# Attention visits of two query blocks in a hybrid convolution and attention step

## Chip, cores and metric

The kernel runs on one core of one Trainium2 chip. The metric is the device time of one execution in microseconds; three executions before gave 949.36, 948.08 and 947.59 (median 948.08). TensorE (PE) does matrix products and transposes, VectorE (DVE), ScalarE (ACT) and GpSimd (POOL) the elementwise work, SyncE (SP) issues most loads. Products land in PSUM, of which a tile of 128 partitions x 512 float32 columns is one bank.

## The reference

One layer for two groups of tokens that share all weights: 128 context tokens ("prompt") and 512 latent tokens on a grid of 8 x 64. Each layer projects its modulated input, runs a gated long convolution (branch A) and attention of 16 heads of 64 channels (branch B), gates, merges and normalises. The change touches branch B alone:

```python
def context_attention(q, k, v):
    s = jnp.einsum("bqhd,bkhd->bhqk", q, k).astype(jnp.float32) * (HEAD_DIM ** -0.5)
    p = jax.nn.softmax(s, axis=-1).astype(v.dtype)
    return jnp.einsum("bhqk,bkhd->bqhd", p, v).reshape(B, L, H * Dh)

def neighbourhood_attention(q, k, v, ctx_k, ctx_v, rpb):
    ...
    s_win = jnp.where(in_win[None, None, None], s_win + bias[None].astype(jnp.float32), NEG_INF)
    s_ctx = jnp.einsum("brqhd,bkhd->bhrqk", qg, ctx_k).astype(jnp.float32) * scale
    p = jax.nn.softmax(jnp.concatenate([s_win, s_ctx], axis=-1), axis=-1).astype(v.dtype)
    o = (jnp.einsum("bhrqk,brkhd->brqhd", p[..., :n_slab], vg)
         + jnp.einsum("bhrqk,bkhd->brqhd", p[..., n_slab:], ctx_v))
    return o.reshape(B, L, H * Dh)
...
p_a = (y_a * jax.nn.silu(g_a)) @ w_ba
```

A latent query sees a window of 16 columns in all 8 grid rows, with a learned bias, and all 128 cached context keys in the same softmax. A context query sees the 128 context keys.

## The kernel before

All work is float32. A weight tile is loaded (`raw`), split by ACT and VectorE into a high and a low part (`wh`, `wl`, L92 and L93), and a projection (`proj`, L154) accumulates three products of 128 x 320 for each of 8 input slices into two PSUM banks (`ps_mm`, two such pairs). One of its steps is 6 matmuls; a projection is 8 steps. The values projection is longer (L680, L689).

Attention goes by pairs of heads, called heads here: `j` = 0 to 7, each of 128 channels, two heads `h` on partitions 0 to 63 and 64 to 127. The latent grid is reordered into 8 blocks of 64 tokens; 128 queries at a time are a query block, `b` = 0 to 3, and `n = 4 j + b` counts query blocks from 0 to 31. The window of a block with its context keys has 320 (b = 0, 3) or 384 columns (b = 1, 2).

- `tiled(n)` (L789) first takes two PSUM tiles `s` and records the scores (L741): for b = 0 also the prompt's, into columns 384 to 511 of the same tiles. Then `probs` (L750): VectorE adds bias and mask and takes the minimum in one custom instruction (L757; the scores are negated, so the minimum is the softmax's maximum), ACT takes the exponential with its sum (L760), VectorE the reciprocal (L761), POOL normalises (L762). The result lies in tiles `p` (5 buffers) or `edge` (b = 0 and 3).
- The same visit then records the values (L785) of block `n - 2`, 6 products for two heads over three chunks of 128 keys, into columns of a PSUM tile `o` that lives for a whole head; with block 0 also the prompt's values into `op`. When block 3 is in, VectorE multiplies `o` with the gate `sg` into `ya` (L839, L840).
- `turned(n)` (L843) transposes the probabilities of block `n - 1` (L778; with block 0 the prompt's, L849) into a PSUM tile `pt` for each head, and ACT copies them to `pts` (L780, L851; 4 buffers).

`s`, `o`, `op`, `pt` and `ptp` all come from `ps_ax`, four banks with one tag `aux`. TensorE's order is that of recording (`manual_schedule`); the other engines' orders and the buffer of each tile are chosen by a scheduler from simulated times. Instructions of different engines on one bank of a tile are kept in recording order.

`weave` (L62) mixes the visits into projections: `attend(j)` yields one visit or transposition, `mains(j)` one projection step, and after each step as many visits follow as the ratio `N_ATT` : `n_main` allows. With 24 steps and `N_ATT` = 8 there is a visit or a transposition after every third step. The projections woven in (`mains`, L889) are those needed two heads later: gate `sg` (two buffers, `gate_a`, L864), queries, keys and values, whose tiles (`slot`) are shared by heads two apart. Head 7 is woven with `mix_h` (L869). After the last gating, ACT and VectorE split all 8 tiles of `yh` and `ya` (L934 and below) for the branch projections.

Of the kernel before, what the change touches and what calls it, by code (L numbers as in the profile page):

```python
# [9 lines left out]
F32 = mybir.dt.float32  # L10
F32R = mybir.dt.float32r
AF = mybir.ActivationFunctionType
ALU = mybir.AluOpType
# [3 lines left out]
LP = 128  # L17
LS = 512
NK = 8
NT = 640  # L20
HALF = 320
PC = 0
SC = 128
B7, B01 = slice(128, 192), slice(192, 320)
# [9 lines left out]
KP = slice(768, 896)  # L34
# [5 lines left out]
def tile_hyena_natten_step(ctx: ExitStack, tc: tile.TileContext, a, o):  # L40
    nc = tc.nc
    P = 128
# [7 lines left out]
    def two(t):  # L50
        return t.rearrange("p (a b) -> p a b", a=2)
# [36 lines left out]
    def aux(name):  # L88
        return ps_ax.tile([P, 512], F32, tag="aux", name=name)
# [81 lines left out]
    out = {"yh": {}}  # L171
# [290 lines left out]
    def quarter_head(q):  # L462
        us = []
        out[f"u{q}"] = us
        for i in range(2):
            n = 2 * q + i
            u = hw.tile([P, NG + 1], F32, tag="u", bufs=4, name=f"u{n}")
            x1 = hwa.tile([P, NG + 1], F32, tag="cv", bufs=2, name=f"x1_{n}")
            yield from conv_tile(n, u)
            yield  # L470
            yield from conv_tile(8 + n, x1)
            nc.vector.tensor_tensor(u[:, :NG], u[:, :NG], x1[:, :NG], op=ALU.mult)
            us.append(u)
            yield
# [142 lines left out]
    def chain(*gens):  # L617
        for g in gens:
            yield from g
# [4 lines left out]
    head = quarter_head(0)  # L624
# [82 lines left out]
    ya, tms, edges, biases = [], [], {}, {}  # L707
# [21 lines left out]
    at = mask = None  # L729

    def bias_tile(hd):
        tb = at.tile([P, 256], F32, tag="tb", bufs=2, name=f"tb{hd}")
        load_to(tb[:], a["rpbT"][hd])
        tm = tms[hd % 4]
        nc.gpsimd.tensor_tensor(tm[:, :192], mask[:, :192], tb[:, 64:], op=ALU.subtract)
        nc.gpsimd.tensor_tensor(two(tm[:, 320:832])[:, :, :P], two(mask[:, 192:448]), two(tb[:]), op=ALU.subtract)
        nc.gpsimd.tensor_tensor(tm[:, 832:], mask[:, 448:], tb[:, :192], op=ALU.subtract)
        return tm

    def score(dst, q, k, h):  # L740
        nc.tensor.matmul(dst, q[rows(h)], k[rows(h)], start=True, stop=True, skip_group_check=True)  # L741
# [8 lines left out]
    def probs(j, b, s, tm):  # L750
        lo, hi = TWIN[b]
        res = []
        for h in range(2):
            p = edges[b, h] if b in (0, 3) else at.tile([P, 384], F32, tag="p", bufs=5, name=f"p{j}_{h}_{b}")
            pv = p[:, LIVE[b]]
            sm = at.tile([P, 3], F32, tag="sm", bufs=8, name=f"sm{j}_{h}_{b}")
            nc.vector.tensor_tensor_reduce(  # L757
                pv, s[h][:, : hi - lo], tm[h][:, lo:hi], 1.0, 3.0e38, ALU.add, ALU.min, accum_out=sm[:, 0:1]
            )
            nc.scalar.activation(pv, pv, AF.Exp, scale=-1.0, bias=sm[:, 0:1], accum_out=sm[:, 1:2])  # L760
            nc.vector.reciprocal(sm[:, 2:3], sm[:, 1:2])  # L761
            nc.gpsimd.tensor_scalar_mul(pv, pv, sm[:, 2:3])  # L762
            res.append(p)
        return res
# [8 lines left out]
    def transposed(j, b, ps):  # L773
        res = []
        for h in range(2):
            pt = aux(f"pt{j}_{h}_{b}")
            for i, (_, c) in enumerate(CHUNKS[b]):
                nc.tensor.transpose(pt[:, i * P : i * P + P], ps[h][:, c : c + P], ident[:])  # L778
            ptS = at.tile([P, 384], F32, tag="pts", bufs=4, name=f"pts{j}_{h}_{b}")
            nc.scalar.activation(ptS[:], pt[:, :384], AF.Copy)  # L780
            res.append(ptS)
        return res

    def pvm(dst, lhs, rhs, start, stop):
        nc.tensor.matmul(dst, lhs, rhs, start=start, stop=stop, skip_group_check=True)  # L785

    head = {}

    def tiled(n):  # L789
        j, b = divmod(n, 4)  # L790
        if n < 4 * NK:
            if b == 0:
                cv = at.tile([P, P], F32, tag="cacheV", bufs=2, name=f"cv{j}")
                load_to(cv[:], a["cv"][:, j * P : j * P + P])
                head[j] = dict(cv=cv, tm=biases.pop(j))
            st_ = head[j]
            s = [aux(f"s{b}_{j}_{h}") for h in range(2)]
            if b == 0:
                for h in range(2):
                    score(s[h][:, 384:512], out[f"q{j}"][:, :LP], out[f"k{j}"][:, KP], h)  # L800
            scores(j, b, s)
            if b == 0:
                pp = st_["pp"] = at.tile([P, 2, P], F32, tag="p", bufs=5, name=f"pp{j}")
                sm = at.tile([P, 3, 2], F32, tag="smp", bufs=2, name=f"smp{j}")
                for h in range(2):
                    nc.vector.tensor_reduce(sm[:, 0, h : h + 1], s[h][:, 384:512], axis=mybir.AxisListType.X, op=ALU.min)
                    nc.scalar.activation(
                        pp[:, h], s[h][:, 384:512], AF.Exp, scale=-1.0, bias=sm[:, 0, h : h + 1], accum_out=sm[:, 1, h : h + 1]
                    )
            st_[b] = probs(j, b, s, st_["tm"])  # L810
            if b == 0:
                nc.vector.reciprocal(sm[:, 2], sm[:, 1])
                for h in range(2):
                    nc.gpsimd.tensor_scalar_mul(pp[:, h], pp[:, h], sm[:, 2, h : h + 1])
            if b == 1 and j + 1 < NK:
                biases[j + 1] = [bias_tile(2 * j + 2 + h) for h in range(2)]
        if n < 2:
            return
        j, b = divmod(n - 2, 4)
        st_, v, sg = head[j], out[f"v{j // 2}"], out[f"sg{j}"]  # L820

        def val(t, h):
            c = 256 * t + P * (j % 2) + 64 * h
            return v[:, c : c + 64]

        if b == 0:
            st_["o"] = aux(f"o{j}")
        ops = st_["o"]
        for i, (t, _) in enumerate(CHUNKS[b]):
            for h in range(2):  # L830
                lhs = st_["cv"][:, rows(h)] if t is None else val(t, h)
                pvm(ops[rows(h), b * P : b * P + P], lhs, st_["t", b][h][:, i * P : i * P + P], i == 0, i == 2)
        if b == 0:
            opp = aux(f"op{j}")
            for h in range(2):
                pvm(opp[rows(h), :P], val(0, h), st_["ptp"][:, h * P : h * P + P], True, True)
            nc.vector.tensor_tensor(ya[j][:, PC : PC + LP], sg[:, PC : PC + LP], opp[:, :P], op=ALU.mult)
        if b == 3:
            nc.vector.tensor_tensor(ya[j][:, B7], sg[:, B7], ops[:, 448:], op=ALU.mult)  # L839
            nc.vector.tensor_tensor(ya[j][:, B7.stop :], sg[:, B7.stop :], ops[:, :448], op=ALU.mult)  # L840
            del head[j]

    def turned(n):  # L843
        j, b = divmod(n - 1, 4)
        st_ = head[j]
        if b == 0:
            pt = aux(f"ptp{j}")
            for h in range(2):
                nc.tensor.transpose(pt[:, h * P : h * P + P], st_["pp"][:, h], ident[:])  # L849
            ptp = st_["ptp"] = at.tile([P, 2 * P], F32, tag="pts", bufs=4, name=f"ptsp{j}")  # L850
            nc.scalar.activation(ptp[:], pt[:, : 2 * P], AF.Copy)  # L851
        st_["t", b] = transposed(j, b, st_[b])

    def attend(j):
        for n in range(4 * j, 4 * j + 4 if j < 7 else 4 * j + 6):
            tiled(n)
            yield
            if 0 < n < 33:
                turned(n)
                yield  # L860

    N_ATT = 8

    def gate_a(j):  # L864
        out[f"sg{j}"] = sg = at.tile([P, NT], F32, tag="sg", bufs=2, name=f"sg{j}") if j else row(yhp, "yh", "sg0")
# [309 lines left out]
```

## Time and profile before

| | us |
|---|---|
| median of three executions | 948.08 |
| profiled execution, its time | 949.61 |
| its span | 947.7 |
| granted TensorE clock, mean | 0.992 |
| attention stage (first to last score or value), about | 401 to 693 |
| in 401 to 693: PE / DVE / ACT / POOL busy | 291.59 / 93.43 / 127.41 / 111.43 |

Some costly groups of the attention stage, by line, engine and operation (busy time, then the mean of one in ns, then idle time before it and what ended it):

```profile
L93 DVE TENSOR_TENSOR wl<-raw,wh 128x1024 fp32r<-128x1024 f32 x31 | 38.4, 1240 | 114.7 <-ACT wh L92 114.7
L757 DVE CUSTOM_DVE_ANT_0 p<-s,tm 128x384 f32<-128x384 f32 x32 | 16.7, 556 | 44.6 <-PE s L741 44.6
L780 ACT ACTIVATE pts<-pt 128x384 f32<-128x384 f32 x64 | 28.0, 491 | 35.9 <-PE pt L778 35.9
L762 POOL TENSOR_SCALAR p<-p,sm 128x384 f32<-128x384 f32 x32 | 43.7, 1376 | 46.8 <-DVE sm L761 46.8
L839 DVE TENSOR_TENSOR ya<-sg,o 128x64 f32<-128x64 f32 x8 | 1.7, 206 | 1.4 <-PE o L785 1.4
L840 DVE TENSOR_TENSOR ya<-sg,o 128x448 f32<-128x448 f32 x8 | 4.9, 615 | 0.0
```

A row of the timeline gives start and duration in us, engine, line, operation, output and inputs, the form (for TensorE the shape of the array part that is used, then the moving operand) and how many like instructions are merged. A float32 score or value product appears as two records, one for each pass.

### The profile page before, as it was taken

Reading aid. Unit: us, or ns where it says so; the run is one execution under the profiler, and the core shown is the slowest. Engines: PE = TensorE matmul, PEld = TensorE weight load, DVE = VectorE, ACT = ScalarE, POOL = GpSimd, SP = SyncE. Lnnn points to the kernel's source line nnn. Section 1 sums busy time; section 2 is a strip of 40 time slices with the busy share of each in tenths; the row PEclk is TensorE's granted clock in tenths of the full one; section 3 lists DMA queues with packets and bytes.
Section 4 is the critical chain, followed back from the end, with each engine's and each line's share of the span. In section 5 each row is a group of like instructions: output and inputs, shape, how many; then the busy total and the mean of one; then the engine's idle time right before and its main releaser. Section 6 shows DMA issues by size and latency. Waiting matters only on the chain.

```text
span 947.7 us, 16408 instructions
## 1 busy us (share of the span) xinstructions
PE 921.4 (97%) x6732; PEld 868.3 (92%) x6732; DVE 469.9 (50%) x839; ACT 375.8 (40%) x759; POOL 153.8 (16%) x190
## 2 busy tenths in 40 slices
PE   5989999999999999999999999999999999999996
PEld 3889999999999999988888889989999999999885
DVE  5548685793795775333333332332271223325686
ACT  3266454554554324254444443443361112223300
POOL 1110010110110000464445544213100000000000
PEclk9899999999999999999999999999999999999999
DMA  8865564555565212322222221221212433223631
GB/s 314 315 174 117 125 142 100 134 133 117 119 141 120 71 56 73 113 80 70 68 74 68 63 68 54 76 70 46 68 52 82 135 133 112 72 84 108 204 111 67
DMA packets 38482, 102.57 MB, mean 108 GB/s; under 512 B 5287, under 2 KB 14951, under 8 KB 38408
## 3 DMA queue, kind: packets, MB, share of 16 engines
q1 hardware_dynamic: 33840, 86.69, 28.9%
q0 software_dynamic: 4032, 14.68, 9.5%
q8 instruction: 53, 0.87, 0.4%
q10 hardware_dynamic: 536, 0.16, 0.1%
q14 instruction: 21, 0.17, 0.1%
HBM read 97.85 MB, written 3.67 MB: 107 GB/s over the span
## 4 chain that ended last, share of the span: by engine, by line
PE 89%; DVE 2%; ACT 1%; DMA 1%; issue 0%; POOL 0%; POOLq 0%; DVEq 0%; ACTq 0%
PE mm L154 62%; PE out L1010 6%; PE v L680 5%; PE s L741 3%; PE o L785 3%; PE pt L778 2%; PE ve L689 1%; DMA raw<-wall 1%; DVE wl L93 1%; PE yb L142 1%; PE yb L143 1%; PE yb L141 1%; PE ut L503 0%; PE fl L365 0%; PE fl L366 0%; ACT wh L92 0%
## 5 line engine op out<-in xcount | busy, mean ns | idle before, releaser
L154 PE MATMUL mm<-hH,wh 128*128 128x320 f32 x1120 | 266.1, 317 | 2.2 <-ACT mh L883 1.1
L154 PE MATMUL mm<-hL,wh 128*128 128x320 f32 x1120 | 259.2, 310 | 2.1 <-POOL hL L93 2.1
L154 PE MATMUL mm<-hH,wl 128*128 128x320 f32 x1120 | 260.3, 311 | 0.8 <-DVE wl L93 0.8
L154 PEld LDWEIGHTS mm<-hH,wh 128*128 128x128 f32 x1120 | 185.9, 189 | 10.8 <-issue 6.9
L154 PEld LDWEIGHTS mm<-hL,wh 128*128 128x128 f32 x1120 | 188.7, 189 | 3.1 <-POOL hL L93 2.7
L154 PEld LDWEIGHTS mm<-hH,wl 128*128 128x128 f32 x1120 | 188.8, 189 | 2.2 <-DVE wl L93 1.6
L93 DVE TENSOR_TENSOR wl<-raw,wh 128x1024 fp32r<-128x1024 f32 x66 | 81.3, 1231 | 194.0 <-ACT wh L92 194.0
L92 ACT ACTIVATE wh<-raw 128x1024 fp32r<-128x1024 f32 x66 | 70.0, 1060 | 178.1 <-PE mm L154 99.6
L133 POOL DMA_DIRECT2D wl<-wall x28 | 24.4, 872 | 230.0 <-ACT wl L132 188.1
L762 POOL TENSOR_SCALAR p<-p,sm 128x384 f32<-128x384 f32 x32 | 43.7, 1376 | 46.8 <-DVE sm L761 46.8
L134 ACT ACTIVATE wh<-raw 128x1024 fp32r<-128x1024 f32 x28 | 29.7, 1062 | 46.6 <-PE mm L154 46.6
L780 ACT ACTIVATE pts<-pt 128x384 f32<-128x384 f32 x64 | 28.0, 491 | 35.9 <-PE pt L778 35.9
L1040 POOL TENSOR_TENSOR r<-r,bc 128x64 f32<-128x64 f32 x1 | 0.3, 319 | 249.5 <-ACT r L1039 249.5
L757 DVE CUSTOM_DVE_ANT_0 p<-s,tm 128x384 f32<-128x384 f32 x32 | 16.7, 556 | 44.6 <-PE s L741 44.6
L760 ACT ACTIVATE p<-p,sm 128x384 f32<-128x384 f32 x32 | 19.5, 612 | 47.0 <-DVE sm L757 47.0
L762 POOL TENSOR_SCALAR edge<-edge,sm 128x320 f32<-128x320 f32 x32 | 34.4, 1085 | 16.0 <-PE mm L154 8.8
L455 DVE SCALAR_TENSOR_TENSOR x<-zs,convw,x 128x641 f32<-128x641 f32 x32 | 28.3, 885 | 5.7 <-ACT x L453 5.6
L132 ACT ACTIVATE wl<-raw 128x1024 fp32r<-128x1024 f32 x28 | 30.1, 1076 | 2.0 <-DMA raw<-wall 2.0
L757 DVE CUSTOM_DVE_ANT_0 edge<-s,tm 128x320 f32<-128x320 f32 x32 | 14.6, 489 | 31.3 <-PE s L741 27.1
L154 PE MATMUL mm<-yhH,wh 128*128 128x320 f32 x128 | 29.9, 315 | 0.0
L741 PE MATMUL s<-k,q 64*128 64x320 f32 (+2 forms) x160 | 29.4, 461 | 0.0
L154 PE MATMUL mm<-yhH,wl 128*128 128x320 f32 x128 | 29.2, 310 | 0.1
(312 smaller groups left out, 1662.6 us busy)
## 6 DMA issues: line engine op xcount, KB each, us to landing
raw<-wall SPq DMA_DIRECT2D x96, 512.0 KB, 3.7
wl<-wall POOLq DMA_DIRECT2D x28, 512.0 KB, 5.7
ada<-wada SPq DMA_DIRECT2D x16, 512.0 KB, 6.3
gate<-wada SPq DMA_DIRECT2D x8, 512.0 KB, 3.7
wo<-wall SPq DMA_DIRECT2D x8, 512.0 KB, 3.7
xt<-xT SPq DMA_DIRECT2D x8, 320.0 KB, 6.6
dec<-decay SPq DMA_DIRECT2D x20, 128.0 KB, 3.4
x<-xB SPq DMA_DIRECT2D x5, 512.0 KB, 5.6
```

Of the source, the lines that this page charges most:

```text
L92: hi = nc.scalar.activation(dst_h, src, AF.Copy)
L93: return hi, (eng or nc.vector).tensor_tensor(dst_l, src, f(dst_h), op=ALU.subtract)
L132: nc.scalar.activation(wl, raw[:], AF.Copy, scale=-1.0)
L134: nc.scalar.activation(wh, raw[:], AF.Copy)
L154: nc.tensor.matmul(ps[hf][:, :HALF], wt[k], x[:, hf * HALF : (hf + 1) * HALF], start=(first and k == 0), stop=(last and k == NK - 1), skip ...
L455: nc.vector.scalar_tensor_tensor(d, zs[:, c : c + NG], convw[:, i, c : c + 1], d, op0=ALU.mult, op1=ALU.add)
L680: nc.tensor.matmul(ps[:, t // 2, t % 2 * 256 : t % 2 * 256 + 256], x[:, k, P * t : P * t + P], wk, start=first and t % 2 == 0, stop=last, ...
L741: nc.tensor.matmul(dst, q[rows(h)], k[rows(h)], start=True, stop=True, skip_group_check=True)
L757: nc.vector.tensor_tensor_reduce(pv, s[h][:, : hi - lo], tm[h][:, lo:hi], 1.0, 3.0e38, ALU.add, ALU.min, accum_out=sm[:, 0:1])
L762: nc.gpsimd.tensor_scalar_mul(pv, pv, sm[:, 2:3])
L785: nc.tensor.matmul(dst, lhs, rhs, start=start, stop=stop, skip_group_check=True)
L1010: ins = nc.tensor.matmul(dst, m[k][:, c0 : c0 + P], w[:, c : c + n], start=(first and k == 0), stop=(last and k == NK - 1), skip_group_che ...
```

## The change

`tiled(i)` now handles two query blocks, `n = 2 i` and `2 i + 1`. It takes four score tiles, records the scores of both blocks (four products, six where the first is block 0; each has two passes, so eight and twelve records), then the values of the blocks `2 i - 4` and `2 i - 3`, then the minimum, exponential and normalisation of the new blocks. The values go into columns 384 to 511 of score tiles (not those with prompt scores), so that there is no tile `o`. Each block's values are gated by themselves. The prompt's values come with blocks 2 and 3 instead of block 0. Two tiles of their own hold the values where no new blocks are left. `turned(i)` transposes two blocks. `pts` has 5 buffers, `N_ATT` is 4.

```diff
-            ptS = at.tile([P, 384], F32, tag="pts", bufs=4, name=f"pts{j}_{h}_{b}")
+            ptS = at.tile([P, 384], F32, tag="pts", bufs=5, name=f"pts{j}_{h}_{b}")
...
+    def gated(j, cols, o_):
+        nc.vector.tensor_tensor(ya[j][:, cols], out[f"sg{j}"][:, cols], o_, op=ALU.mult)
+
+    def block_values(n, o_):
+        j, b = divmod(n, 4)
+        for i, (t, _) in enumerate(CHUNKS[b]):
+            for h in range(2):
+                lhs = head[j]["cv"][:, rows(h)] if t is None else val(j, t, h)
+                pvm(o_[rows(h)], lhs, head[j]["t", b][h][:, i * P : i * P + P], i == 0, i == 2)
+        if b < 3:
+            gated(j, slice(192 + P * b, 320 + P * b), o_)
+        else:
+            gated(j, slice(576, NT), o_[:, :64])
+            gated(j, B7, o_[:, 64:])
+
+    def prompt_values(j, o_):
+        for h in range(2):
+            pvm(o_[rows(h)], val(j, 0, h), head[j]["ptp"][:, h * P : h * P + P], True, True)
+        gated(j, slice(PC, PC + LP), o_)
+
+    def tiled(i):
+        ns = [n for n in (2 * i, 2 * i + 1) if n < 4 * NK]
+        ss = {n: [aux(f"s{n}_{h}") for h in range(2)] for n in ns} or {0: [aux(f"ov{i}_{h}") for h in range(2)]}
+        spare = [t[:, 384:] for n, pair in ss.items() if n % 4 or not ns for t in pair]
+        for n in ns:
+            block_scores(n, ss[n])
+        for n in (2 * i - 4, 2 * i - 3):
+            if n >= 0:
+                block_values(n, spare.pop(0))
+        j, b = divmod(2 * i - 4, 4)
+        if b == 2 and j >= 0:
+            if not spare:
+                spare.append(aux(f"op{j}")[:, 384:])
+            prompt_values(j, spare.pop(0))
+            del head[j]
+        for n in ns:
+            block_probs(n, ss[n])
+
+    def turned(i):
+        for n in (2 * i - 2, 2 * i - 1):
...
+            st_["t", b] = transposed(j, b, st_[b])
 
     def attend(j):
-        for n in range(4 * j, 4 * j + 4 if j < 7 else 4 * j + 6):
-            tiled(n)
+        for i in range(2 * j, 2 * j + 2 if j < 7 else 2 * j + 4):
+            tiled(i)
             yield
-            if 0 < n < 33:
-                turned(n)
+            if 0 < i < 17:
+                turned(i)
                 yield
 
-    N_ATT = 8
+    N_ATT = 4
```

`block_scores` and `block_probs` hold what `tiled` did for one block before, cut in two: loading the cached values and the score products, and `probs` with the prompt's softmax and the next head's bias tiles.

More of the change, by code (lines that the diff above doesn't have):

```diff
@@ L787, in tile_hyena_natten_step, with block_scores @@
     head = {}
-    def tiled(n):
+    def block_scores(n, s):
         j, b = divmod(n, 4)
[L791 to L824, printed above, removed]
-        if b == 0:
-            st_["o"] = aux(f"o{j}")
-        ops = st_["o"]
@@ new lines, in block_scores, with block_probs @@
+        if b == 0:
+            cv = at.tile([P, P], F32, tag="cacheV", bufs=2, name=f"cv{j}")
+            load_to(cv[:], a["cv"][:, j * P : j * P + P])
+            head[j] = dict(cv=cv, tm=biases.pop(j))
+            for h in range(2):
+                score(s[h][:, 384:512], out[f"q{j}"][:, :LP], out[f"k{j}"][:, KP], h)
+        scores(j, b, s)
+    def block_probs(n, s):
+        j, b = divmod(n, 4)
+        st_ = head[j]
+        if b == 0:
+            pp = st_["pp"] = at.tile([P, 2, P], F32, tag="p", bufs=5, name=f"pp{j}")
+            sm = at.tile([P, 3, 2], F32, tag="smp", bufs=2, name=f"smp{j}")
+            for h in range(2):
+                nc.vector.tensor_reduce(sm[:, 0, h : h + 1], s[h][:, 384:512], axis=mybir.AxisListType.X, op=ALU.min)
+                nc.scalar.activation(
+                    pp[:, h], s[h][:, 384:512], AF.Exp, scale=-1.0, bias=sm[:, 0, h : h + 1], accum_out=sm[:, 1, h : h + 1]
+                )
+        st_[b] = probs(j, b, s, st_["tm"])
+        if b == 0:
+            nc.vector.reciprocal(sm[:, 2], sm[:, 1])
+            for h in range(2):
+                nc.gpsimd.tensor_scalar_mul(pp[:, h], pp[:, h], sm[:, 2, h : h + 1])
+        if b == 1 and j + 1 < NK:
+            biases[j + 1] = [bias_tile(2 * j + 2 + h) for h in range(2)]
@@ L829, in tiled, with val @@
+    def val(j, t, h):
+        c = 256 * t + P * (j % 2) + 64 * h
+        return out[f"v{j // 2}"][:, c : c + 64]
+    def gated(j, cols, o_):
+        nc.vector.tensor_tensor(ya[j][:, cols], out[f"sg{j}"][:, cols], o_, op=ALU.mult)
+    def block_values(n, o_):
+        j, b = divmod(n, 4)
         for i, (t, _) in enumerate(CHUNKS[b]):
             for h in range(2):
-                lhs = st_["cv"][:, rows(h)] if t is None else val(t, h)
-                pvm(ops[rows(h), b * P : b * P + P], lhs, st_["t", b][h][:, i * P : i * P + P], i == 0, i == 2)
@@ L833, in tiled @@
[L833 to L840, printed above, removed]
-            del head[j]
@@ L843, in turned @@
[L843 to L852, printed above, removed]
+                lhs = head[j]["cv"][:, rows(h)] if t is None else val(j, t, h)
@@ new lines, in turned @@
+    def turned(i):
+        for n in (2 * i - 2, 2 * i - 1):
+            j, b = divmod(n, 4)
+            st_ = head[j]
+            if b == 0:
+                pt = aux(f"ptp{j}")
+                for h in range(2):
+                    nc.tensor.transpose(pt[:, h * P : h * P + P], st_["pp"][:, h], ident[:])
+                ptp = st_["ptp"] = at.tile([P, 2 * P], F32, tag="pts", bufs=5, name=f"ptsp{j}")
+                nc.scalar.activation(ptp[:], pt[:, : 2 * P], AF.Copy)
+            st_["t", b] = transposed(j, b, st_[b])
```

1 line of the change is left out of this document (added).

## The prediction

> **What bounds the kernel now.** I read the page first, then the list of waits of TensorE over the attention stage, then the PE timeline of single attention visits, then the other engines around them.
>
> ```profile
> span 947.7 us, 16408 instructions
> PE 921.4 (97%) x6732; PEld 868.3 (92%) x6732; DVE 469.9 (50%) x839; ACT 375.8 (40%) x759; POOL 153.8 (16%) x190
> PE 89%; DVE 2%; ACT 1%; DMA 1%; issue 0%; POOL 0%; POOLq 0%; DVEq 0%; ACTq 0%
> ```
>
> TensorE is busy 97% of the span and holds 89% of the chain that ended last; its granted clock is 0.992. So only TensorE time counts, and a busy TensorE can hide slow starts. Its waits from 401 us (first attention scores) to 707 us are nearly nothing:
>
> ```profile
> PE mm L154 <- ACT mh L883: 1.1, 1, 1.1
> PE mm L154 <- DVE wl L93: 0.8, 3, 0.3
> ```
>
> Three visits of the PE timeline (start, busy, line, tile). In a visit TensorE leaves the projection (L154), runs scores (L741) and values (L785), and goes back.
>
> ```profile
> 412.20 0.46 PE L154 MATMUL mm<-hH,wl 128*128 128x320 f32 x2
> 412.59 0.92 PE L741 MATMUL s<-k,q 64*128 64x384 f32 x4
> 413.44 0.66 PE L785 MATMUL o<-pts,v 128*64 128x128 f32 x8
> 413.93 0.39 PE L785 MATMUL o<-pts,cv 128*64 128x128 f32 x4
> 414.14 0.39 PE L785 MATMUL op<-ptsp,v 128*64 128x128 f32 x4
> 414.46 0.56 PE L154 MATMUL mm<-hH,wh 128*128 128x320 f32 x2
> 414.86 0.46 PE L154 MATMUL mm<-hL,wh 128*128 128x320 f32 x2
> ```
> ```profile
> 420.60 0.81 PE L741 MATMUL s<-k,q 64*128 64x320 f32 x4
> 421.34 0.66 PE L785 MATMUL o<-pts,v 128*64 128x128 f32 x8
> ```
> ```profile
> 430.92 1.03 PE L741 MATMUL s<-k,q 64*128 64x128 f32 x8
> 431.88 0.66 PE L785 MATMUL o<-pts,v 128*64 128x128 f32 x8
> ```
>
> Starts, not busy times, tell the cost, since matmuls overlap. From score start to value start: 0.74 us for one block of 320 columns, 0.85 for 384, 0.96 where 128 prompt columns precede 320. The two heads run side by side and each call makes two passes (four records for two calls), so the columns streamed are 640, 768 and 896. Each 128 columns more add 0.11 us, and 640 columns leave 0.74 - 5 x 0.11 = 0.19 us over. That rest is the same with one call per head and with two: it is paid per visit, not per call. This is what the prediction rests on.
>
> **The change part by part.** *Visits.* Before, blocks 0 to 31 each have a score visit and values follow two blocks later: 2 visits with scores alone, 30 with both, 2 with values alone. After, with two blocks each and values two visits later: 2, 14 and 2. The matmuls stay as many and as long. So 16 passages through scores and values go. Fixed price of one, from the first visit:
> - L154 to scores: 412.59 - 412.20 = 0.39; undisturbed rows of two start 0.29 apart (the row before this one starts at 411.91): 0.10 over.
> - scores to values: the 0.19 above.
> - start of values: four passes take 0.49, the next two 0.21, so 0.07 over 4 x 0.105.
> - values to L154: 414.46 - 414.14 = 0.32, against 0.21: 0.11.
> - first L154 row: 0.40 against 0.29: 0.11.
> Whole visit as a check: 414.86 - 412.20 = 2.66, less 2 x 0.29, 6 x 0.11 (columns) and eight passes at 0.105, leaves 0.58, as the pieces do. With starts rounded to 0.01 this is good to 0.04, mostly on the high side (passes of 0.105 to 0.11); I take 0.55. 16 x 0.55 = 8.8 us gained.
>
> The Trainium skill, "TensorEngine Tiling (Array Packing)", section Tiling Modes, says that a change of tiling mode, and not of the tile alone, drains TensorE. The rows agree: the shapes in the rows are `64*128`, `128*64` and `128*128`, and each entry costs, a second call in one shape nothing. The page gives no figure; by it 16 x 3 = 48 changes go, by the rows at 0.55 / 3 each.
>
> *Transposes.* Their visits fall from 32 to 16 too:
>
> ```profile
> 416.92 0.46 PE L154 MATMUL mm<-hH,wl 128*128 128x320 f32 x2
> 417.21 0.82 PE L778 MATMUL pt<-ident,p 128*128 128x128 f32 x6
> 417.79 0.54 PE L154 MATMUL mm<-hH,wh 128*128 128x320 f32 x2
> 418.16 0.45 PE L154 MATMUL mm<-hL,wh 128*128 128x320 f32 x2
> ```
>
> They are entered 0.29 after the last row, as any row is, and the way out takes 0.58 + 0.37 for six transposes at 0.11 and a row of 0.29: nothing over. Gain 0 (bounds 0 and 16 x 0.05).
>
> *Gating.* VectorE multiplies the values in six pieces a head, not three: before 0.206 + 0.615 + 0.281, after four of 0.281 and two of 0.206, +0.43 us a head. VectorE is busy 93 of 292 us in this stage; TensorE covers it. Cost 0; without cover 8 x 0.43 = 3.4.
>
> *PSUM banks.* Four `aux` banks. Now one double visit fills all four with scores; the transposes that follow 36 matmuls (36 x 0.147 = 5.3 us; 0.147 is half a row) later need four, or five with the prompt's. The long tile `o` is gone. Banks come free when VectorE has gated and taken its minima. In the visit at 430.92 its two edge minima end at 434.03 and the reciprocals at 435.05, behind a weight split of 1.23. Now two gatings (0.28 each) and two minima (0.47 apart) come behind: about 436.5. The visit itself grows to about 3.3 us, so ends at 434.2, and the transposes are due at 439.5: 3 us of margin. The fifth transposed tile takes the bank of the first, the prompt's: ACT copies that in 0.383 (`ptsp`), so it is free at about 0.11 + 0.272 (one transpose's own time) + 0.383 + 0.1 for two handovers = 0.9 us, needed at 11 x 0.11 = 1.2. If ACT is inside a weight copy (1.06) it is late by up to 0.7; eight such bursts: 0 to 5.6 us. The weave puts the weight and q/k copies (together 2.3 to 2.5 us) 2.6 us ahead, so I take 0.3 in all.
>
> *Semaphores.* 33 PE instructions instead of 9 wait for three things; the extra wait instruction takes 0.051 (eleven at L741 now, with the entry still 0.39). Bounds 0 and 24 x 0.051 = 1.2; I take 0, as at L741.
>
> *Gate buffer.* `sg` has two buffers; gate 3 writes that of gate 1. Gate 1's last reader moves from the 7th to the 13th of head 2's 24 projection steps, gate 3 is ready to be written at the 8th, and the projection at the 17th needs gate 3's bank. From the visit's end to that need: 18 x 0.147 = 2.7 us. Behind the last gating come ACT's tanh (0.683, behind two exps of 0.61) and VectorE's 0.812, behind minima: about 3.0. Cost 0.3, once (bounds 0 and 2).
>
> *The end of attention.* There the two waits of TensorE lie:
>
> ```profile
> 703.80 0.46 PE L154 MATMUL mm<-hH,wl 128*128 128x320 f32 x2
> 705.38 0.56 PE L154 MATMUL mm<-hH,wh 128*128 128x320 f32 x2 [1.13 <-ACT mh L883]
> 705.78 0.45 PE L154 MATMUL mm<-hL,wh 128*128 128x320 f32 x2
> 706.50 0.56 PE L154 MATMUL mm<-hH,wl 128*128 128x320 f32 x2 [0.27 <-DVE wl L93]
> 706.90 0.31 PE L154 MATMUL mm<-hH,wh 128*128 128x320 f32 x1
> ```
>
> 703.80 to 706.90 are four rows, 1.17 us at pace: 1.93 lost. Sixteen splits of yh and ya keep ACT from 693.53 to 703.71 once the last gating is done. After the change the last values stand 12 matmuls (1.8 us) earlier in the projection, and a gating of 0.28 instead of 0.206 + 0.615 follows the last matmul; so the splits start some 2.3 us earlier against TensorE's need. Gain 1.9 (bounds 0 and 1.93).
>
> **Sum.** -8.8 - 1.9 + 0.3 + 0.3 = -10.1 us. The profiled execution took 949.61 (span 947.7), 1.53 above the median of 948.08. So 939.5 profiled, and 938.0 as median.
>
> **The rivals.**
> - *The price sticks to the block.* If the first pass of each block's scores and values pays again (half of the 0.19, and the 0.07), a visit saves 0.55 - 0.17 = 0.38: 6.1 + 1.9 - 0.6 = 7.4 gained, 940.7. Against it: the 128-then-320 visit, which pays once. Chance 0.08.
> - *The end keeps its wait*, because a load or another order holds the sixteen splits: 8.8 - 0.6 = 8.2, 939.9. Chance 0.14.
> - *New waits eat half*: the fifth tile late by 0.5 in all eight prompt bursts (4) and gate 3 late by 1: 10.7 - 5 = 5.7, 942.4. For it: four banks for five tiles; against it the margins above. Chance 0.11.
> - *Slower: bank starvation.* A minimum now also waits for the values written beside its scores (as in the visit at 430.92 an edge minimum waited 0.50 for ACT's exps of the prompt columns in its bank), and reciprocals that wait for ACT stand between the minima. If VectorE's last minimum comes over 3.0 us later than reckoned, every transposing visit waits; at 3.7 the gain is used up (16 x 0.67 = 10.7). At 4 it is 16 x 1.0 = 16: 948.1 - 10.7 + 16 = 953.4. It would need a weight split (1.24), a gate (0.812) and a full set of k copies with a weight copy (2.5) ahead of the chain in nearly every visit; the page's 50% and 40% speak against. Chance 0.04. The Trainium skill, "PSUM — Partial Sum Buffer", on bank collisions, says that two engines may not touch one bank and quadrant at once, whatever the columns; the 0.50 agrees; no row before shows values beside scores.
>
> **How the numbers follow.** My forecast has 0.62, centre 938.0, own range 936.8 to 939.5. The rivals at 939.9, 940.7 and 942.4 lie on one side, so the range reaches to 942.5 and, with no extra wait and timing noise of the runs (947.59 to 949.36), down to 936.6. About 0.2% (1.9 us) is what a measurement of this kernel can tell from no change. Forecast and first three rivals are faster by more (0.95, of which I leave 0.02 to something unseen that lands near zero); slower 0.05.
>
> **What would show it.** PE rows: about 18 attention visits, each still with 0.39 into scores, 0.19 over between scores and values, 0.40 for the first L154 row; within a visit the second block's scores follow at 0.11 per 128 columns. PE waits over 1 us at transposes, named after DVE or ACT, would show the bank rivals; at the projection after gate 3, the buffer; idle near 695 to 700 us, the end. Wrong would be a visit whose overhead grows with its blocks, or DVE idle on reciprocals in front of minima while TensorE waits.

## The result and the profile after

| | before | after |
|---|---|---|
| median of the executions | 947.84 us (947.46 to 949.36, 4) | 937.7 us (937.23 to 938.28, 4) |
| profiled execution, its time | 949.61 us | 938.28 us |
| its span | 947.7 us | 936.4 us |
| granted TensorE clock, mean | 0.992 | 0.995 |
| first score product to first output product (L1010 before, L1028 after) | 481.74 us | 471.38 us |

The changed kernel is faster: ratio 0.9894, 95% interval 0.9879 to 0.9908. The forecast was 938.0 with a range of 936.6 to 942.5.

Of the 11.3 us between the two spans, 0.96 lie ahead of the first score (401.58 us before, 400.62 after). The change has no part in that: over all profiled executions of this study the first score lies between 398.7 and 402.8. So I compare the *stretch* from the start of the first score product to the start of the first output product. It holds all that the change touches, and two more profiled executions of the changed kernel give 471.06 and 471.08.

The page of the changed kernel (busy time, share and instructions of each engine; the chain that ended last by engine):

```profile
PE 912.5 (97%) x6732; PEld 869.6 (93%) x6732; DVE 469.3 (50%) x863; ACT 373.3 (40%) x759; POOL 149.9 (16%) x190
...
PE 89%; DMA 2%; DVE 1%; ACT 1%; issue 0%; SPq 0%; POOLq 0%; POOL 0%; ACTq 0%
```

TensorE has the same 6732 matmuls and still 89% of the chain; its busy time is 8.9 us less. No other engine has come into the chain. The list of TensorE's waits from 401 to 707 us (total, times, longest):

```profile
PE mm L154 <- DVE wl L93: 0.3, 1, 0.3
PE mm L154 <- DVE sm L761: 0.2, 1, 0.2
```

The wait for ACT's `mh` is gone and a short new one is there. One double visit on the PE timeline, with the scores of blocks 2 and 3 (384 and 320 columns for each of two heads), two blocks of values and the prompt's:

```profile
471.91 0.45 PE L154 MATMUL mm<-hH,wl 128*128 128x320 f32 x2
472.29 1.45 PE L741 MATMUL s<-k,q 64*128 64x384 f32 x8
473.67 0.66 PE L785 MATMUL s<-pts,v 128*64 128x128 f32 x8
474.16 0.39 PE L785 MATMUL s<-pts,cv 128*64 128x128 f32 x4
474.38 0.61 PE L785 MATMUL s<-pts,v 128*64 128x128 f32 x8
474.81 0.39 PE L785 MATMUL s<-pts,cv 128*64 128x128 f32 x4
475.03 0.39 PE L785 MATMUL s<-ptsp,v 128*64 128x128 f32 x4
475.35 0.56 PE L154 MATMUL mm<-hH,wh 128*128 128x320 f32 x2
```

The way in costs 0.38, as before; scores to values take 1.38, which for 1408 columns at 0.11 per 128 leaves 0.17 over, once for the whole visit and not per block; the second block of values (474.38) starts 0.22 after the `cv` row ahead of it, the pace of two passes, with nothing extra. So a double visit pays once what each of two single visits paid.

The transposes come late enough for the banks. After fifteen of the sixteen visits with scores the next burst of transposes begins 3.2 to 9.9 us after VectorE's last minimum of that visit, after one 1.87 us. The lines: the last minimum of the visit above (VectorE timeline), and, in another visit, a burst of twelve transposes (PE timeline):

```profile
476.62 0.49 DVE L757 CUSTOM_DVE_ANT_0 edge<-s,tm 128x320 f32<-128x320 f32 x1
```
```profile
465.61 0.82 PE L778 MATMUL pt<-ident,p 128*128 128x128 f32 x6
466.26 0.82 PE L778 MATMUL pt<-ident,edge 128*128 128x128 f32 x6
466.83 0.55 PE L154 MATMUL mm<-hH,wh 128*128 128x320 f32 x2
```

The minimum ends at 477.11, 1.8 us after the projection has gone on (475.35); the burst takes 466.83 - 465.61 = 1.22 for twelve transposes, no wait in it.

At the end of attention (ACT and PE timelines):

```profile
682.03 5.13 ACT L92 ACTIVATE yhH<-yh 128x640 fp32r<-128x640 f32 x8 [1.72 <-DVE ya L823]
687.07 5.12 ACT L92 ACTIVATE yaH<-ya 128x640 fp32r<-128x640 f32 x8
...
693.14 0.68 ACT L901 ACTIVATE mh<-mm 128x640 f32<-128x640 f32 x1
```
```profile
694.72 0.45 PE L154 MATMUL mm<-hH,wh 128*128 128x320 f32 x2
695.01 0.46 PE L154 MATMUL mm<-hL,wh 128*128 128x320 f32 x2
```

The sixteen splits run from 682.03 to 687.07 + 5.12 = 692.19, and the copy of `mh` behind them (L901 here, L883 before) is out at 693.82. TensorE's rows stand 0.29 apart throughout, and the wait of before is gone.

Gaps between projection rows beyond the pace of 0.147 us per matmul, summed over the stretch, are 2.81 us before and 1.32 after (1.01 in both repeats).

### The profile page after: what moved, and what is told of

Its sections match the earlier page's. It is cut to its first block, busy times and chain, and to the rows that moved or that the text cites. A ratio compares the mean times of both kernels' runs of the same rounds, so it can differ in the third digit from the quotient of the medians.

```text
span 936.4 us, 16384 instructions
## 1 busy us (share of the span) xinstructions
PE 912.5 (97%) x6732; PEld 869.6 (93%) x6732; DVE 469.3 (50%) x863; ACT 373.3 (40%) x759; POOL 149.9 (16%) x190
## 4 chain that ended last, share of the span: by engine, by line
PE 89%; DMA 2%; DVE 1%; ACT 1%; issue 0%; SPq 0%; POOLq 0%; POOL 0%; ACTq 0%
PE mm L154 62%; PE out L1028 6%; PE v L680 5%; PE s L741 3%; PE pt L778 2%; PE s L785 2%; DMA raw<-wall 2%; PE ve L689 1%; ACT wh L92 1%; DVE wl L93 1%; PE yb L143 1%; PE yb L142 1%; PE yb L141 1%; PE ut L503 1%; PE fl L365 0%; PE fl L366 0%
## 5 line engine op out<-in xcount | busy, mean ns | idle before, releaser
L154 PE MATMUL mm<-hH,wh 128*128 128x320 f32 x1120 | 263.0, 314 | 1.0 <-ACT v L692 0.7
L762 POOL TENSOR_SCALAR p<-p,sm 128x384 f32<-128x384 f32 x32 | 41.8, 1317 | 28.7 <-DVE sm L761 28.7
L154 PE MATMUL mm<-yhL,wh 128*128 128x320 f32 x128 | 29.2, 309 | 0.0
L154 PE MATMUL mm<-yaL,wh 128*128 128x320 f32 x128 | 29.1, 308 | 0.0
L154 PE MATMUL mm<-yaH,wh 128*128 128x320 f32 x128 | 29.1, 308 | 0.0
```

The source lines that it names most:

```text
L154: nc.tensor.matmul(ps[hf][:, :HALF], wt[k], x[:, hf * HALF : (hf + 1) * HALF], start=(first and k == 0), stop=(last and k == NK - 1), skip ...
```

## The experiments

Each changes a few lines of the changed kernel, one of the kernel before. All were timed against the kernel before on the same chip.

| | median, us | kernel before, us | ratio to before, 95% interval | stretch, us |
|---|---|---|---|---|
| changed kernel again | 937.66 | 947.46 | 0.9893, 0.9876 to 0.9909 | 471.06 |
| 1 mixed order | 952.05 | 947.46 | 1.0052, 1.0036 to 1.0068 | 486.20 |
| 2 mixed order without the shared bank | 943.52 | 947.31 | 0.9961, 0.9948 to 0.9975 | 476.32 |
| 3 values apart from scores | 940.85 | 947.46 | 0.9929, 0.9916 to 0.9941 | 475.42 |
| 4 transposes one block at a time | 937.34 | 947.46 | 0.989, 0.9876 to 0.9904 | 470.82 |
| 5 the end alone, in the kernel before | 945.57 | 947.7 | 0.9978, 0.9968 to 0.9988 | 479.89 |
| 6 transposes at once | 950.97 | 947.7 | 1.0043, 1.0029 to 1.0057 | 485.41 |
| 7 three gate buffers | 937.95 | 947.7 | 0.9902, 0.9888 to 0.9915 | 470.64 |
| 8 three gate buffers, fewer modulation visits | 935.17 | 947.7 | 0.9872, 0.9857 to 0.9887 | 469.34 |
| changed kernel, third time | 937.55 | 947.31 | 0.9893, 0.9877 to 0.9909 | 471.08 |
| 8 again | 936.09 | 947.31 | 0.9875, 0.9857 to 0.9893 | 469.35 |

**The changed kernel again.**

> The changed kernel once more, beside the others of this group as their yardstick. It should give about 937.7 us, 10.1 under the kernel before (0.9894), and in its trace the same visits: 0.38 to 0.39 us into the scores and 0.40 for the first projection row after the values. Nothing is told apart by it.

It repeats, and its stretch agrees to 0.3 us. The third time:

> The changed kernel once more, on the same chip as the combined version, for a direct comparison: 937.7 us (937.0 to 938.5).

**1. Mixed order.** Inside a double visit scores and values alternate by block, so that TensorE goes from the score shape to the value shape twice.

```diff
-        for n in ns:
-            block_scores(n, ss[n])
-        for n in (2 * i - 4, 2 * i - 3):
-            if n >= 0:
-                block_values(n, spare.pop(0))
+        for m in range(2):
+            if m < len(ns):
+                block_scores(ns[m], ss[ns[m]])
+            if 2 * i - 4 + m >= 0:
+                block_values(2 * i - 4 + m, spare.pop(0))
```

> The changed kernel with the order in a visit of two blocks changed to scores, values, scores, values; as many visits, the same products. Theory (the price is paid at each change of the shape in which the array is used): each of the 14 visits that have both gets two changes more, back to the scores (0.10 on entry and 0.10 at their first pass) and again to the values (0.09 and 0.05), 0.35 us in all, so 14 x 0.35 = 4.9 us slower than the changed kernel: about 942.6. First rival (the price is paid for leaving the projection, once a visit): no change, 937.7. Second rival (the price sticks to each block): no change either, for it would be paid already.

This missed by far: the stretch grew by 15.1 us over the changed kernel. Two effects were mixed. The visits without a block 0 took 3.42 us from the first score to the projection instead of 3.06, the expected 0.36. The seven others lost much more. One of them on the PE and the VectorE timeline:

```profile
426.22 0.39 PE L785 MATMUL s<-pts,cv 128*64 128x128 f32 x4
428.08 0.92 PE L741 MATMUL s<-k,q 64*128 64x384 f32 x4 [1.47 <-DVE ya L823]
```
```profile
424.80 1.23 DVE L93 TENSOR_TENSOR wl<-raw,wh 128x1024 fp32r<-128x1024 f32 x1 [5.77 <-ACT wh L92]
425.94 0.48 DVE L806 TENSOR_REDUCE smp<-s 128x1 f32<-128x128 f32 x2
...
427.34 0.49 DVE L757 CUSTOM_DVE_ANT_0 edge<-s,tm 128x320 f32<-128x320 f32 x1
...
427.75 0.28 DVE L823 TENSOR_TENSOR ya<-sg,s 128x128 f32<-128x128 f32 x1
```

Where block 0's tiles have no free columns, the edit put the values into the tiles of the second block, ahead of that block's scores. Instructions on one bank keep their recorded order, so the scores waited until VectorE had gated the values out of the other columns of the bank. That gating stood on VectorE behind a weight split, the prompt's minima and two edge minima, and ended at 428.03; the scores started at 428.08. TensorE's waits for it come to 9.7 us in seven waits (longest 1.6), and 15.1 - 14 x 0.37 (the price of experiment 2) is 9.9.

**2. Mixed order without the shared bank.** The same alternation, but in visits with a block 0 the second block's scores go first.

```diff
-        for n in ns:
+        for m, n in enumerate(ns if i % 2 else ns[::-1]):
             block_scores(n, ss[n])
-        for n in (2 * i - 4, 2 * i - 3):
-            if n >= 0:
-                block_values(n, spare.pop(0))
+            if i > 1:
+                block_values(2 * i - 4 + m, spare.pop(0))
+        for n in (2 * i - 4, 2 * i - 3) if not ns else ():
+            block_values(n, spare.pop(0))
```

> The same order as in the mixed run (scores, values, scores, values inside a visit, so TensorE changes between the score shape and the value shape twice more in each of 14 visits), but in the visits that hold a block 0 the other block's scores now come first, so that no score product follows values into the bank that VectorE still has to read for the gating. Theory (two effects in the mixed run: a price for every change of shape, read there as about 0.36 us a visit in the seven visits without a wait, and a wait for the gating in the other seven): 14 x 0.35 = 4.9 us over the changed kernel, so about 942.5 us (941.5 to 943.5), and no TensorE wait named after VectorE's gating. Rival (the mixed run's loss was general, VectorE being behind in every mixed visit): 947 us or more. Other rival (the price is paid once a visit, however often the shape changes): about 937.7.

The stretch is 476.32 - 471.08 = 5.24 us longer, 0.374 for each of 14 visits, where 0.35 was expected; no wait for the gating is left. The median, 943.52, lies just above the expected 941.5 to 943.5. A visit of it on the PE timeline:

```profile
428.83 0.92 PE L741 MATMUL s<-k,q 64*128 64x384 f32 x4
429.67 0.66 PE L785 MATMUL s<-pts,v 128*64 128x128 f32 x8
430.16 0.39 PE L785 MATMUL s<-pts,cv 128*64 128x128 f32 x4
430.48 1.03 PE L741 MATMUL s<-k,q 64*128 64x128 f32 x8
431.44 0.66 PE L785 MATMUL s<-pts,v 128*64 128x128 f32 x8
431.93 0.39 PE L785 MATMUL s<-pts,cv 128*64 128x128 f32 x4
432.25 0.57 PE L154 MATMUL mm<-hH,wh 128*128 128x320 f32 x2
```

The same matmuls, with five changes of shape in place of three: each change costs 0.374 / 2 = 0.19 us, and 0.554 / 3 = 0.18 in the changed kernel. So the price hangs on the change of shape and not on the visit, the block or the call. Nor is it a price of the two passes: scores and values both take two, so the added changes, between scores and values, are of the shape and not of the number of passes. The Trainium skill, "TensorEngine Tiling (Array Packing)", section Tiling Modes, says that a change of mode drains TensorE and a change of tile alone does not; the runs agree, with 0.18 to 0.19 us for a change and nothing for a further product in the same shape. That the time goes into a drain is not shown here.

**3. Values apart from scores.** One projection step of six matmuls goes between the scores and the values of a visit (in 12 of 14 visits), which adds one change of shape.

```diff
             block_scores(n, ss[n])
+        yield
...
-            tiled(i)
-            yield
+            yield from tiled(i)
+            for _ in range(5):
+                yield
             if 0 < i < 17:
                 turned(i)
-                yield
+                for _ in range(6):
+                    yield
 
-    N_ATT = 4
+    N_ATT = 24
...
-            weave(chain(*main), attend(j), n_main, N_ATT if j < 7 else N_ATT + 3)
+            weave(chain(*main), attend(j), n_main, N_ATT if j < 7 else N_ATT + 18)
```

> The changed kernel with one projection step (six products) between the scores and the values of a visit, in 12 of the 14 visits that have both. Theory: a visit with scores alone costs 0.39 and one with values alone 0.34 (rows of the kernel before at 405.38 and 691.74), one with both 0.55, so 12 x 0.18 = 2.2 us slower; the last values stand six products later (0.9 us), which may bring back some 0.2 of the wait at the end: about 940.1. Rival (paid for leaving the projection): 12 leavings more at 0.55 are 6.6 us: 944.3. Rival (nothing of the kind, the gain came from elsewhere): 937.7.

One such visit on the PE timeline:

```profile
440.50 1.45 PE L741 MATMUL s<-k,q 64*128 64x384 f32 x8
441.88 0.56 PE L154 MATMUL mm<-hH,wh 128*128 128x320 f32 x2
...
442.95 0.66 PE L785 MATMUL s<-pts,v 128*64 128x128 f32 x8
```

The median comes out 0.75 above what was expected, and the stretch says why: of its 4.34 us (against 471.08), 12 x 0.198 = 2.38 are the changes of shape, as theory had it, and 1.95 are longer gaps between projection rows (2.96 instead of 1.01). Of these, 0.88 is the wait of gate 3 (1.22 instead of 0.34; experiment 7 tells what this row waits for in the changed kernel), since the last reader of gate 1 now comes six matmuls later:

```profile
478.61 0.53 PE L154 MATMUL mm<-hH,wh 128*128 128x320 f32 x2 [1.06 <-DVE sm L761]
```

The others are short, the largest two late weight splits (0.55 at 697.6 us and 0.31 at 766.8). The time of the change hangs on where values stand, not only on how many visits there are.

**4. Transposes one block at a time.** `turned` is split again into 32 visits; scores and values stay double.

```diff
     def turned(i):
         for n in (2 * i - 2, 2 * i - 1):
+            if n % 2:
+                for _ in range(3):
+                    yield
...
             if 0 < i < 17:
-                turned(i)
-                yield
+                yield from turned(i)
+                for _ in range(3):
+                    yield
```

with the ratios of the weave in sixths as in experiment 3.

> The changed kernel with its transposes in visits of one block again, 32 instead of 16, with projection steps between; scores and values as in the changed kernel. Theory: transposes use the array in the projection's shape and cost nothing on entry or exit, so within 0.3 us of the changed kernel, 937.7. Rival (any interruption of the projection costs its share, and half of the interruptions that went were transposes): 16 x 0.27 = 4.4 us slower, 942.1.

One of the added visits on the PE timeline:

```profile
438.27 0.81 PE L778 MATMUL pt<-ident,edge 128*128 128x128 f32 x6
438.84 0.54 PE L154 MATMUL mm<-hH,wh 128*128 128x320 f32 x2
439.22 0.45 PE L154 MATMUL mm<-hL,wh 128*128 128x320 f32 x2
```

From 438.27 to 439.22 there are 0.95 us, for six transposes at 0.11 and a row of 0.29: nothing over. The stretch differs by -0.26 us for 16 more visits with transposes, and 0.2 of this is a burst of fourteen that is late in the changed kernel and not here. The added visits cost nothing: they have the projection's shape, 128*128.

**5. The end alone, in the kernel before.** The ratio of the last head's weave is raised, so that its values come earlier against the projection, with no other edit.

```diff
-            7: ((mix_h(),), 7 * NK),
+            7: ((mix_h(),), 7 * NK - 3),
```

> The kernel before with one number changed, the ratio by which the last head's visits are woven: the last values stand 12 products (1.76 us) earlier in the projection, where the changed kernel has them. Visits and their shapes stay. Theory: the wait of TensorE at the end of the attention stage (1.93 us from 703.80 to 706.90) goes or nearly goes, because the sixteen splits start 1.76 us earlier against it: 1.5 to 1.9 us under the kernel before, about 946.0. Rival (that wait has another cause, or comes back behind the splits): no change, 947.8.

The stretch falls by 1.85, all of it in the gaps between projection rows (2.81 to 0.96). Of this, 1.53 lies at the end of attention; the other 0.32 is a weight split that was late at 775 us in the kernel before and is not here, which the edit does not explain. The rows where 1.13 and 0.27 were waited before are the first and the third of these:

```profile
702.11 0.46 PE L154 MATMUL mm<-hH,wh 128*128 128x320 f32 x2
702.40 0.46 PE L154 MATMUL mm<-hL,wh 128*128 128x320 f32 x2
703.00 0.56 PE L154 MATMUL mm<-hH,wl 128*128 128x320 f32 x2
```

What is left is 0.60 from 702.40 to 703.00 in place of 0.29, a weight split. So most of the end's share of the gain (1.53 of 1.94) is had without double visits, by one number.

**6. Transposes at once.** The transposes of two blocks follow the values directly, which takes all cover from the four banks.

```diff
             tiled(i)
-            yield
             if 0 < i < 17:
                 turned(i)
-                yield
+            yield
 
-    N_ATT = 4
+    N_ATT = 2
...
-            weave(chain(*main), attend(j), n_main, N_ATT if j < 7 else N_ATT + 3)
+            weave(chain(*main), attend(j), n_main if j < 7 else 8 * NK, N_ATT if j < 7 else N_ATT + 2)
```

> The changed kernel with the transposes right behind the values of the visit instead of six projection steps later, so that they want the four score banks while VectorE still takes the minima. In the changed kernel's trace the last minimum ends 2.2 us after the visit where it has 12 score records and 1.8 where it has 8, and the transposes come 3.2 to 7.2 us after that. Theory (four banks, 3 us of cover): now the last tile waits for that minimum, 1.4 us in each of 7 visits, and 0.8 to 2 in each of 8 visits whose fifth tile also waits for ACT's copy of the first, behind its exps: 16 to 26 us slower than the changed kernel, 954 to 964, slower than the kernel before. Rival (the banks decide nothing): 937.7.

It is slower than before, as the fourth rival says of starved banks. The list of TensorE's waits, its largest:

```profile
PE pt L778 <- DVE sm L757: 6.8, 14, 0.9
```

The stretch is 14.3 us longer, less than the 16 to 26 expected. Bursts of twelve transposes take 2.62 instead of 1.23 us, bursts of fourteen 2.03 instead of 1.45: those that follow a visit with a block 0 wait longer, because its minima end about 2.2 us after its last matmul and the others' 1.6.

**7. Three gate buffers.** The short wait in the changed kernel's list (a row of the PE timeline, which stands 0.63 behind the one ahead of it where 0.29 is the pace; then ACT and VectorE):

```profile
478.43 0.53 PE L154 MATMUL mm<-hH,wh 128*128 128x320 f32 x2 [0.18 <-DVE sm L761]
```
```profile
476.75 0.68 ACT L459 ACTIVATE sg<-mm 128x640 f32<-128x640 f32 x1
...
477.47 0.82 DVE L460 SCALAR_TENSOR_TENSOR sg<-sg,mm 128x640 f32<-128x640 f32 x1 [0.21 <-ACT sg L459]
```

The row is put down to a reciprocal (L761), which reads nothing that the row needs. The bank that the row needs is that of gate 3, and its last reader, L460, ends at 478.29 (the expectation below gives this time as the row's start, which is 478.43). To tell the two apart, `sg` gets a third buffer:

```diff
-        out[f"sg{j}"] = sg = at.tile([P, NT], F32, tag="sg", bufs=2, name=f"sg{j}") if j else row(yhp, "yh", "sg0")
+        out[f"sg{j}"] = sg = at.tile([P, NT], F32, tag="sg", bufs=3, name=f"sg{j}") if j else row(yhp, "yh", "sg0")
```

> The changed kernel with a third buffer for the gate tile alone. Theory: the row that started 0.49 us after the one before it (478.29 in the changed kernel's trace, named after VectorE) starts after 0.15, the rest stays: 0.34 us less, not more than the runs can tell, 937.4; the trace decides. Rival (the wait was for the projection's weight, or for a bank that the minima hold): the row still starts late.

The wait is gone, and the stretch is 0.42 to 0.44 shorter than in the two repeats of the changed kernel, which is all of that wait. The medians can't tell a difference of this size (937.95 against 937.7). It was the gate buffer, not the reciprocal.

**8. Three gate buffers and fewer modulation visits.** The price of a shape should be paid by any product that differs from its neighbours. After attention eight groups of modulation products stand alone in the branch projections, in a fourth shape (128*32). Two at a time make four visits:

```diff
-                raw = wp.tile([P, D], F32, tag="raw", name=f"gate{pair}{i}")
-                ada(16 + 4 * pair + i, ps[:, i * P : i * P + P], raw[:])
+                ch, dst = 16 + 4 * pair + i, ps[:, i * P : i * P + P]
+                if i % 2 == 0:
+                    raw = wp.tile([P, D], F32, tag="raw", name=f"gate{pair}{i}")
+                    ada(ch, dst, raw[:])
+                    continue
+                for t in range(2):
+                    half = slot(1, "qk"[t], f"gate{pair}{i}{t}")[:, :512]
+                    load_to(half, a["wada"][ch][:, 512 * t : 512 * t + 512])
+                    for j in range(4):
+                        nc.tensor.matmul(
+                            dst[32 * j : 32 * j + 32, :], st[:, 4 * t + j, :], half[:, P * j : P * j + P],
+                            start=(t == 0), stop=(t == 1), skip_group_check=True, tile_position=(0, 32 * j),
+                        )
                 yield
...
-        next(side, None)
+        if n % 2:
+            next(side, None)
```

> The changed kernel with two edits drawn from the theory: a third buffer for the gate tile, which takes away the 0.34 us wait at the projection after gate 3, and the gate products of the end (128 rows by 32 columns, a fourth shape) in four visits of 16 products instead of eight of 8, the second operand of each pair in memory that is free by then. A visit of 8 costs 0.33 us by the rows (0.09 on entry, 0.03 at the first pass, 0.11 on exit, 0.10 at the first projection row). Theory: 4 x 0.33 + 0.34 = 1.7 us under the changed kernel, 936.0. Rival (a load of the second operand comes late, or a weight behind it): a wait in its place, 937.7 or more.

One visit in the changed kernel, then one of the second try of this experiment ("8 again"; PE timeline):

```profile
715.54 0.46 PE L154 MATMUL mm<-yhH,wl 128*128 128x320 f32 x2
715.92 0.65 PE L235 MATMUL gate<-gate,st 128*32 128x128 f32 x16
716.50 0.56 PE L154 MATMUL mm<-yhH,wh 128*128 128x320 f32 x2
```
```profile
723.80 0.64 PE L235 MATMUL gate<-gate,st 128*32 128x128 f32 x16
724.26 0.62 PE L946 MATMUL gate<-gate,st 128*32 128x128 f32 x16
724.81 0.56 PE L154 MATMUL mm<-yhH,wh 128*128 128x320 f32 x2
```

The second group adds 0.43 (1.01 from start to projection, against 0.58). From the row ahead (715.54) to the second row behind (716.90) a single group takes 1.36, which is 0.77 over two rows at pace; less 0.43 for the products, 0.34 is the price of the two changes of shape. Four visits fewer should be 4 x 0.34 = 1.4 us; the stretch is 1.30 less than in experiment 7.

> The version with three gate buffers and the modulation products in fewer visits once more, on the same chip as the changed kernel: 1.7 to 2.5 us below it, about 935.5 us. If the earlier gain was the chips' scatter, it is within 1 us of it.

On one chip the medians are 936.09 and 937.55, 1.46 apart where 1.7 to 2.5 was expected, with executions that overlap (933.56 to 937.28, and 936.37 to 938.25); the stretch is 1.73 less, as in the first try. The stretch shows the gain; the medians alone would not settle it.

## Why the prediction was right

The mechanism was the one forecast: a passage through scores and values has a fixed price, 16 passages went, and the wait at the end went with them. The stretch of the kernel before, 481.74, less that of the undisturbed repeat, 471.08, is 10.66 us, to be compared with the 10.1 of the sum. Less that of the profiled execution of the result, 471.38, it is 10.36; that execution has a late weight split of 0.32 that the kernel before has too and the repeat has not. That the median, 937.7, lies 0.3 us from the forecast is in part luck: executions of the changed kernel alone scatter by 1 us, and small terms on both sides cancel. The terms, for the 10.66:

| step of the prediction | reckoned, us | shown, us |
|---|---|---|
| visits, 16 passages | -8.8 | -8.86 (what is left of 10.66 when the 1.80 of the gaps are taken off; the late bursts of the third row lie in it and cancel) |
| end of attention | -1.9 | -1.94 (gaps of 1.29 + 0.11 + 0.43 + 0.11 at 705.4 to 706.8, now 0) |
| four banks, five tiles | +0.3 | +0.2 (one burst of fourteen at 1.66 instead of 1.45; the same in the repeat), against -0.2 for a burst of six that was late in the kernel before (0.80 instead of 0.57 at 515.62) |
| gate buffer | +0.3 | +0.42 (experiment 7) |
| transposes | 0 | about 0 (experiment 4) |
| semaphores | 0 | 0: the ways in and out of a visit are those of before |

- **Visits.** The reading that the fixed price is paid per visit and not per call was right for a reason that the prediction only touched: it is paid per change of shape. 8.86 / 16 = 0.554 against 0.55. Experiments 2 and 3 price a change alone (0.19 and 0.20), and three of them in a passage give 0.55 to 0.6.
- **The price sticks to the block** (rival): excluded by the double visit's rows, where the second block starts with nothing extra.
- **The end keeps its wait** (rival): it did not, and experiment 5 shows that the earlier position of the last values against the projection is enough for 1.53 of the 1.94. The prediction's reason, a start of the splits some 2.3 us earlier, holds nearly in size: they begin 0.62 us after TensorE has left its last values (681.41), where it was 0.98 before (692.55), which with the 1.76 of the 12 matmuls is 2.1. In experiment 5 they begin 1.23 after, so 1.5 earlier, and a weight split is still late by 0.41.
- **New waits eat half** (rival): both places showed, small. The burst with the fifth tile was late once in eight, by 0.2, in the way the prediction describes: its twelfth transpose, the first into the fifth tile, starts at 617.66, and ACT's copy of the prompt's tile, which stood behind a weight copy and the copies of the keys, ends at 617.52. The gate buffer's wait was reckoned at 0.3 and took 0.42; a later place of the values makes it 1.3 (experiment 3), so this margin is thin.
- **Bank starvation** (rival): the mechanism is real (experiment 6 is slower than the kernel before) and the cover holds it off. The prediction put the last minimum about 2.3 us after the visit and the transposes 5.3 us after it; the traces have 1.5 to 2.5 and 5.4 or more, but for one visit with 3.6. Its price without any cover was set too high in my expectation: 14.3 us.
- **Gating.** Nothing of its six pieces reached TensorE, and VectorE's busy time over the span is 469.3 after 469.9. The cover is what matters: in experiment 1, where a score product was queued behind a gating, it cost 9.9 us.
- **Outside the sum.** A weight split was late by 0.32 at 775 us before and at 764 in one execution after, and not in the two repeats; it makes the difference between 10.36 and 10.66. I found no cause in the change for it. Most of the rest between sum and stretch is the burst of the kernel before that is no longer late, for which the sum had no term.
- **Median.** The sum was set against the profiled execution: 939.5 forecast, 938.28 measured, of which 0.96 is the earlier first score.

## What to carry to other kernels

Where TensorE sets the time, read its cost from the starts of its rows and look for what is paid at a change of the array shape: here 0.17 to 0.20 us each, whatever follows in the new shape, so that putting small products of one shape together gains and alternating them loses. Products that share a PSUM bank with values which another engine still reads are ordered behind that reader; free columns of a bank are a gift only where nothing else has to be written into the bank soon. After such a merge ask for the cover, not for busy shares: it was the projection matmuls between a visit and the transposes, 36 or more but once, that kept the gain, and without them the same change was slower than before.

## What the runs showed that I had not expected

- Free columns of a bank that is soon written again let TensorE wait for VectorE's whole queue (experiment 1), 1.4 us a time, though VectorE is busy for only half of the span.
- The releaser that the trace names can be a neighbour: the gate buffer's wait was put down to a reciprocal of 0.15 us that began 0.09 us before its real releaser ended.
- Modulation products of shape 128*32, 16 records of 128 columns, pay 0.34 us a visit, nearly half of what they cost in all; transposes, in the projection's shape, pay nothing.
